# Expert weights passed in 4 MB buffers with a part of all 16 experts each, and 28 blocks of slots instead of 32

## The chip, the cores and the metric

The kernel runs on one core of a Trainium2 chip. Its engines are TensorE (PE, with its weight loads shown apart as PEld), VectorE (DVE), ScalarE (ACT), GpSimd (POOL) and SyncE (SP, which here only issues DMAs). Matmul results land in PSUM (8 banks of 2 KB for each of 128 partitions), everything else sits in SBUF, and all weights come from HBM by DMA. The metric is the device time of one execution in microseconds (us), lower is better.

## The reference, cut to what matters

Two layers act on 256 tokens of width 1024, in fp32. Each layer is a modulated mixer (convolution and two kinds of attention) and a mixture of 16 experts:

```python
for l in range(2):
    mod = silu(c) @ w_ada[l] + b_ada[l]             # 1024 -> 6 x 1024
    sh1, sc1, g1, sh2, sc2, g2 = split(mod, 6)
    h = rms_norm(x, g_mix[l]) * (1 + sc1) + sh1
    x = x + g1 * token_mixers(h, ...)               # w_in: 1024 -> 2340, w_o: 1024 -> 1024
    h = rms_norm(x, g_ffn[l]) * (1 + sc2) + sh2
    aff = sigmoid(h @ w_router); gates = top 2 of 16 experts, both of the best group of 4, normed
    x = x + g2 * sum_e gates[:, e] * ((silu(h @ w_gate[l, e]) * (h @ w_up[l, e])) @ w_down[l, e])
return rms_norm(x, g_final)
```

w_gate and w_up are [2, 16, 1024, 256], w_down is [2, 16, 256, 1024]: 50.3 MB for each layer. Of 256 tokens, 512 pairs of token and expert are routed; an expert can get any number of them. On the inputs that are timed the experts' counts, in units of 32 tokens, exceed one block each for some and two blocks for few.

## The kernel before, in words

**Weights.** All big weight loads stand in one list, `loads`, in the order in which TensorE will use them. `pump` (L72) walks it: while fewer than RING = 14 pieces are issued and not yet freed, it takes a 1 MB tile of the ring and issues the piece's DMAs on SP's queue (L77). `done` (L81) frees a piece after its last matmul and calls `pump` again. The list (L131 to L153) has, for layer 0: sc1 and sh1 (two of the six 4 MB column groups of w_ada, four pieces each), the columns of w_in, g1, sh2, sc2, w_o, g2, then sc1 of layer 1, then the experts, then sh1 of layer 1. An expert load is for a pair of experts: four gate/up pieces of four DMAs of 256 KB (contiguous rows of 1 KB in HBM) and two w_down pieces of two DMAs of 512 KB (rows of 2 KB).

**Order.** The order of the instructions on PE, DVE and ACT is the program's order. `Fill` objects hold matmuls of w_ada (L274, 32 columns of weights and 512 columns wide) that are put into places where TensorE would wait; `take(n)` emits n of its pieces.

**Router.** `route` (L727) forms logits, picks two experts by arithmetic on DVE (L746 to L790), writes the selection `slb`, which TensorE turns into ranks and counts `pk` (L803 to L807). Meanwhile ACT writes the normalised tokens `gH` (rounded) and GpSimd the remainder `gL` (L800). From ranks DVE makes keys `ky`, and a flag per pair.

**Experts.** Slots are in blocks of 32 tokens. A pair of experts has a 128-slot tile of four blocks: block 0 belongs to whichever of the two needs it (its weights are selected by a register, `bass.ds(fr[pr], 1)`, L948), block 1 to the first, blocks 2 and 3 to the second. Eight pairs make 32 blocks. For two pairs at a time, `onehot` (L909) makes the one-hot matrix D, `gather` (L927, matmuls L935) collects the tokens into XT, `weigh` and `onehot_T` (L918) the gate-weighted transpose DT. For each pair, `expert_up` (L951) runs 8 x 4 matmuls with gate and up weights side by side, 512 columns wide (L957; each shows as two instructions), `silu_mul` and `act_T` follow, `expert_down` (L989) runs 2 x 2 x 4 matmuls 512 wide (L995), `put_down` evicts, and `combine` (L1002, matmuls L1016 in the last layer and L1022 in the other) adds the pair's output to PSUM sums. While one pair is in `expert_up`, the DVE, ACT and POOL work of another is under way.

**Overflow.** At the end an `If` (L1169) on a register runs slow extra passes if any pair has more tokens than slots. It stands on PE, ACT, DVE and POOL ahead of the last pair's `combine`; on the timed inputs nothing in it runs. Behind it in layer 0 come the residual and the norm of layer 1 (`nnorm`, with the matmuls of sh1 between), in layer 1 `finish` (L1196: squares, root, scaling, output DMA).

Of the kernel before, what the change touches and what calls it, by code (L numbers as in the profile page):

```python
# [9 lines left out]
F32 = mybir.dt.float32  # L10
# [9 lines left out]
P = 128  # L20
# [13 lines left out]
TAKE = (5, 2)  # L34
# [8 lines left out]
RING = 14  # L43
# [9 lines left out]
def block_kernel(ctx: ExitStack, tc: tile.TileContext, x, c, w_ada, b_ada, g_mix, w_in, w_dw, b_dw, ln_conv_g,  # L53
# [16 lines left out]
    loads, wt, issued, freed = [], {}, [0], [0]  # L70

    def pump(most=RING):  # L72
        while issued[0] < len(loads) and issued[0] - freed[0] < most:
            key, shape, parts = loads[issued[0]]
            t = ring.tile(shape, F32, tag="w", name=f"w{issued[0]}")
            for dst, src in parts(t):
                nc.sync.dma_start(out=dst, in_=src)  # L77
            wt[key] = t
# [32 lines left out]
    def moe_src(l, pr, nm, h, n=2):  # L111
        r = slice(h * (DM // n), (h + 1) * (DM // n))
        if nm == "d":
            src = w_down[l, 2 * pr:2 * pr + 2, :, r].rearrange("e (k p) n -> p e k n", p=P)
        else:
            w = w_gate if nm == "g" else w_up
            src = w[l, 2 * pr:2 * pr + 2, r, :].rearrange("e (k p) f -> p e k f", p=P)
        return [src[:, e] for e in range(2)]

    def add_moe(l):  # L120
        for pr in range(NE // 2):
            for h in range(4):
                srcs = [moe_src(l, pr, nm, h, 4) for nm in "gu"]
                loads.append((("gu", l, pr, h), [P, 2, 2, 2, FE],
                              lambda t, srcs=srcs: [(t[:, e, :, w], srcs[w][e]) for e in range(2) for w in range(2)]))
            for h in range(2):
                srcs = moe_src(l, pr, "d", h)
                loads.append((("d", l, pr, h), [P, 2, 2, 512],
                              lambda t, srcs=srcs: [(t[:, e], srcs[e]) for e in range(2)]))
# [37 lines left out]
    desc4 = cp.tile([P, 4], F32, name="desc4")  # L167
    low4 = cp.tile([P, 4, 4], F32, name="low4")
# [28 lines left out]
    pump(10)  # L197
# [13 lines left out]
    nc.sync.dma_start(out=ropet, in_=rope)  # L211
    nc.sync.dma_start(out=wr[:, :, 0:NE], in_=w_router.rearrange("(k p) e -> p k e", p=P))
    nc.sync.dma_start(out=brt, in_=bass.AP(tensor=b_router.tensor, offset=b_router.offset, ap=[[0, P], [1, NE]]))
    pump()
    G.memset(causal, 0.0)
    for lo in (0, 2 * P):
# [8 lines left out]
           allow_small_or_imprecise_dtypes=True)  # L225
    G.iota(desc4, pattern=[[-1, 4]], base=4, channel_multiplier=0, allow_small_or_imprecise_dtypes=True)
# [89 lines left out]

    class Norm:
# [3 lines left out]
        def tile(self, k):  # L321
            if self.wk is None or k < 2:
                return sm.tile([P, SEQ], F32, name="sq", tag="sq", bufs=2)
            if k >= 6:
                return self.wk.tile([P, FE], F32, name="sq", tag="eac", bufs=2)
            if k % 2 == 0:
                self.two = self.wk.tile([P, 2, SEQ], F32, name="sq", tag="yf")
            return self.two[:, k % 2, :]
# [71 lines left out]
    def mixers(big, wk, l, norm, early):  # L400
# [319 lines left out]
        nxt = Fill([(l, "g2"), (l + 1, "sc1")]) if l + 1 < DEPTH else Fill([(l, "g2")], rows=True)  # L720
# [5 lines left out]

    def route(wk, router, xtp, gH, gL, fill):  # L727
# [3 lines left out]
        part = wk.tile([P, SEQ], F32, name="part", tag="eth", bufs=1)  # L731
# [12 lines left out]
        for t in range(NT):  # L744
# [32 lines left out]
        gtr, eql = (wk.tile([P, FE], F32, name=n, tag="eac")[:, 0:8 * 16].rearrange("p (g a b) -> p g a b", g=8, a=4)  # L777
                    for n in ("gtr", "eql"))
# [4 lines left out]
        ct = wk.tile([P, FE], F32, name="ct", tag="eth", bufs=1)[:, 0:32].rearrange("p (g e) -> p g e", e=4)  # L783
# [7 lines left out]
        fill(2)  # L791
        for h in range(2):
            for t in range(NT):
                hs = slice(h * 512, (h + 1) * 512)
                if t == 0:
                    xs2 = wk.tile([P, NT, 512], F32, name="xs", tag="Yh")
                xs = xs2[:, t, :]
                S.activation(xs, xtp[h, t], AF.Copy, scale=rst[:, t:t + 1])
                S.copy(gH[:, t, hs], xs)
                G.tensor_tensor(gL[:, t, hs], xs, gH[:, t, hs].bitcast(F32), OP.subtract)  # L800
# [7 lines left out]
        npair = NE // 2  # L808
        cnt2 = pk[:, 2, :].rearrange("p (q b) -> p q b", b=2)
        f = tmp([P, npair], "f")  # L810
        V.tensor_scalar(f, cnt2[:, :, 0], BLK + 0.5, None, OP.is_lt)
        fi = wk.tile([1, npair], I32, name="fi", tag="fi", bufs=1)
        V.tensor_copy(fi, f[0:1, :])
# [3 lines left out]
        rk2 = rk.rearrange("p t (q b) -> p t q b", b=2)  # L817
        ky = tmp([P, NT, npair, 4], "ky")
        a32 = tmp([P, NT, npair], "a32", "hi")
        fb = f[:, None, :].to_broadcast([P, NT, npair])  # L820
        V.tensor_scalar(a32, rk2[:, :, :, 0], float(-BLK), None, OP.add)
        dl = tmp([P, NT, npair], "dl", "lo")
        V.scalar_tensor_tensor(out=dl, in0=rk2[:, :, :, 1], scalar=float(-2 * BLK), in1=a32, op0=OP.add,
                               op1=OP.subtract)
        V.tensor_tensor(dl, dl, fb, OP.mult)
        V.tensor_tensor(ky[:, :, :, 0], dl, a32, OP.add)
        V.tensor_copy(ky[:, :, :, 1:3], rk2)
        V.tensor_scalar(ky[:, :, :, 3], rk2[:, :, :, 1], float(-BLK), None, OP.add)

        def gates():  # L830
# [9 lines left out]
            gt2 = gt.rearrange("p t (q b) -> p t q b", b=2)  # L840
            gy = tmp([P, NT, npair, 4], "gy")
            V.tensor_copy(gy[:, :, :, 1:3], gt2)
            V.tensor_copy(gy[:, :, :, 3], gt2[:, :, :, 1])
            nf = tmp([P, npair], "nf", "m1")
            V.tensor_scalar(nf, f, -1.0, 1.0, OP.mult, OP.add)
            V.tensor_tensor(dl, gt2[:, :, :, 1], fb, OP.mult)
            V.tensor_tensor(a32, gt2[:, :, :, 0], nf[:, None, :].to_broadcast([P, NT, npair]), OP.mult)
            V.tensor_tensor(gy[:, :, :, 0], dl, a32, OP.add)
            return gt, gy


        def flags():
            fl = wk.tile([1, 3 * npair + 1], I32, name="flags", tag="flags", bufs=1)
            nb = tmp([P, npair], "nb", "m2")
            V.tensor_scalar(nb, f, float(-BLK), None, OP.mult)
            mx = tmp([1, npair], "mx", "m3")
            V.tensor_tensor(mx, cnt2[0:1, :, 1], nb[0:1, :], OP.add)
            V.tensor_tensor(mx, mx, cnt2[0:1, :, 0], OP.max)
            for ch in range(3):
                V.tensor_scalar(fl[:, ch * npair + 1:(ch + 1) * npair + 1], mx, CAP * (ch + 1) + 0.5, None, OP.is_gt)  # L860
            m1x = tmp([1, 1], "m1x")
            V.tensor_reduce(m1x, mx, AX.X, OP.max)
            V.tensor_scalar(fl[:, 0:1], m1x, CAP + 0.5, None, OP.is_gt)
            return fl, nb

        return ky, gates, flags, rk, fi

    def moe(big, wk, l, router, nxt, nnorm):
        a2, sh2 = mod["sc2", l], mod["sh2", l]
        npair = NE // 2  # L870
        last = l + 1 == DEPTH
        if last:

            g2b = big.tile([P, DM], F32, name="g2b")
            o2 = l * 6 * DM + UNITS.index("g2") * DM
            nc.sync.dma_start(out=g2b, in_=bass.AP(tensor=b_ada.tensor, offset=b_ada.offset + o2,
                                                   ap=[[0, P], [1, DM]]))
        g2ps = []

        def spread_g2():  # L880
            for h in range(2):
                pb = bank([P, 512])
                T.matmul(pb, selu[:, 0, h:h + 1].to_broadcast([P, P]), nxt.groups[0].ev, start=True, stop=True)
                g2ps.append(pb)

        gH = big.tile([P, NT, DM], F32R, name="gH")
        gL = big.tile([P, NT, DM], F32R, name="gL")
        xtp = {}

        def fill(i):  # L890
            if i > 1:
                nxt.take(TAKE[i - 2])
                if i == 3 and last:
                    spread_g2()
                return
            for h, t in ((0, 0),) if i == 0 else ((0, 1), (1, 0), (1, 1)):
                pt = bank([P, 512])
                for j in range(4):
                    xk = xT[:, 4 * h + j, t * P:(t + 1) * P]
                    if last:  # L900
# [408 lines left out]
```

## Time and profile before

| | before |
|---|---|
| median of 3 runs | 592.75 us (591.54 to 592.85) |
| profiled execution, time | 592.18 us |
| profiled execution, span | 590.5 us |
| PE busy | 548.6 us, 93% |
| DVE busy | 277.8 us, 47% |
| ACT / POOL busy | 157.6 us, 27% / 46.0 us, 8% |
| DMA moved | 182.82 MB, mean 310 GB/s; SP's queue 88.2% of 16 engines' span |

The span runs from the first to the last record of the execution, and the time is 1.68 us longer. Times below are us from the span's start. The stages of the span: layer 0's mixers to about 159, its router to 181, its experts to 296, the overflow branch, residual and norm to 314; layer 1's mixers to 438.8, its router to 460.2, its experts to 575.2, then the end. In a row, "idle before <-releaser" is the time for which the engine stood still just before the instruction, and what ended it; a name that ends in q (PEq) is that engine's instruction queue.

### The profile page before, as it was taken

To read this page: it belongs to the slowest core of one execution; us is meant where nothing else is said; L and a number is where in the kernel's file an instruction comes from. 1 tells how busy PE (TensorE), PEld (TensorE's weight loads), DVE (VectorE), ACT (ScalarE), POOL (GpSimd) and SP (SyncE) were. 2 spreads that over 40 slices of the span, in tenths; PEclk is the share of its full clock that TensorE was granted. 3 is DMA by queue.
4 is the path that set the end of the run, shared out by engine and by line. 5 is a ranking of instruction groups with operands and counts; after the bars stand their busy time and mean duration, and the time that the engine had idled before them with its cause. 6 is when DMAs were issued, how large, how long until landed. Compare 5 with 4: busy or idle time off the path is not lost. (4 is left out here: it accounts for less than half of the span.)

```text
span 590.5 us, 10358 instructions
## 1 busy us (share of the span) xinstructions
PE 548.6 (93%) x3881; PEld 336.7 (57%) x3881; DVE 277.8 (47%) x882; ACT 157.6 (27%) x368; POOL 46.0 (8%) x51
## 2 busy tenths in 40 slices
PE   2889999999979999999969999999997999999993
PEld 0378886677735444444337788668774554444331
DVE  1321999574264433332133099956427533333222
ACT  1331103346242111111134021344624211111114
POOL 1000004000030000000000000500003011111110
PEclk9979999999989999999979999999998999999997
DMA  8999989973499999999999997957349699999932
GB/s 320 383 302 380 401 316 394 398 268 116 140 335 363 363 363 354 359 348 359 391 352 372 384 383 308 347 196 246 122 143 332 199 360 361 359 363 361 356 112 75
DMA packets 126025, 182.82 MB, mean 310 GB/s; under 512 B 7920, under 2 KB 94216, under 8 KB 125960
## 3 DMA queue, kind: packets, MB, share of 16 engines
q1 hardware_dynamic: 125344, 180.80, 88.2%
q10 hardware_dynamic: 616, 1.19, 0.5%
q8 instruction: 36, 0.59, 0.4%
q14 instruction: 29, 0.24, 0.1%
HBM read 180.92 MB, written 1.05 MB: 308 GB/s over the span
## 5 line engine op out<-in xcount | busy, mean ns | idle before, releaser
L957 PE MATMUL bank<-w,XT 128*32 128x512 f32 (+1 forms) x1024 | 112.9, 592 | 0.0
L431 PE MATMUL bank<-w,hT 128*128 128x256 f32 (+1 forms) x448 | 102.9, 390 | 1.1 <-ACT hT L407 1.1
L431 PEld LDWEIGHTS bank<-w,hT 128*128 128x128 f32 x448 | 85.6, 193 | 16.9 <-ACT hT L407 2.1
L957 PEld LDWEIGHTS bank<-w,XT 128*32 128x32 f32 x1024 | 33.6, 110 | 75.1 <-issue 69.3
L995 PE MATMUL bank<-w,eaT 128*32 128x512 f32 (+1 forms) x512 | 58.2, 595 | 0.4
L645 PE MATMUL bank<-yT,w 128*128 128x256 f32 x256 | 57.5, 381 | 0.0
L274 PE MATMUL bank<-w,cB 128*32 128x512 f32 x384 | 50.8, 641 | 5.7 <-DMA w<-in_w_ada 3.5
L645 PEld LDWEIGHTS bank<-yT,w 128*128 128x128 f32 x256 | 48.0, 190 | 6.8 <-issue 0.7
L674 DVE SCALAR_TENSOR_TENSOR cvy<-cva,hw,cvy 128x256 f32<-128x256 f32 x108 | 49.7, 509 | 0.6
L945 DVE SCALAR_TENSOR_TENSOR eac<-eth,bank 128x256 f32<-128x256 f32 x16 | 6.7, 421 | 83.5 <-ACT eth L944 83.5
L935 PE MATMUL bank<-D,gH 128*128 128x256 f32 x128 | 33.1, 297 | 2.4 <-DVE eac L945 2.4
L995 PEld LDWEIGHTS bank<-w,eaT 128*32 128x32 f32 x512 | 15.2, 110 | 32.0 <-issue 28.9
L944 ACT ACTIVATE eth<-bank 128x256 f32<-128x256 f32 x16 | 6.1, 384 | 96.2 <-PE bank L957 96.2
L935 PE MATMUL bank<-D,gL 128*128 128x256 f32 x128 | 31.2, 282 | 0.0
L939 ACT ACTIVATE XT<-bank,sh,sc 128x256 f32<-128x256 f32 x36 | 18.2, 560 | 44.4 <-PE bank L935 44.4
L935 PEld LDWEIGHTS bank<-D,gH 128*128 128x128 f32 x128 | 24.7, 193 | 6.7 <-issue 4.7
L446 PE MATMUL bank<-hT,w 128*128 128x256 f32 x128 | 28.3, 379 | 0.0
L446 PEld LDWEIGHTS bank<-hT,w 128*128 128x128 f32 x128 | 24.2, 190 | 3.3
L274 PEld LDWEIGHTS bank<-w,cB 128*32 128x32 f32 x384 | 10.6, 112 | 26.7 <-issue 16.5
L983 POOL TENSOR_TENSOR Yl<-yf,Yh 128x512 fp32r<-128x512 f32 x14 | 18.0, 1283 | 95.1 <-ACT Yh L982 95.1
L522 ACT ACTIVATE pr<-pr,nm 128x128 f32<-128x128 f32 (+1 forms) x48 | 21.3, 444 | 14.1 <-DVE nm L519 14.1
L935 PEld LDWEIGHTS bank<-D,gL 128*128 128x128 f32 x128 | 24.7, 193 | 0.2 <-issue 0.2
(268 smaller groups left out, 662.9 us busy)
## 6 DMA issues: line engine op xcount, KB each, us to landing
w<-in_w_ada SPq DMA_DIRECT2D x48, 1024.0 KB, 11.6
w<-in_w_gate SPq DMA_DIRECT2D x128, 256.0 KB, 6.1
w<-in_w_up SPq DMA_DIRECT2D x128, 256.0 KB, 5.9
w<-in_w_down SPq DMA_DIRECT2D x64, 512.0 KB, 7.5
w<-in_w_in SPq DMA_DIRECT2D x16, 1024.0 KB, 13.0
w<-in_w_o SPq DMA_DIRECT2D x8, 1024.0 KB, 9.1
w<-in_w_in SPq DMA_DIRECT2D x4, 328.0 KB, 15.8
xin<-in_x ACTq DMA_DIRECT2D x1, 1024.0 KB, 9.4
```

The lines of the kernel that those rows point to most:

```text
L274: T.matmul(self.pa[j:j + 32, :], cB[:, 2 * kq + kk, o:o + 32], W[:, kk, h * 512:(h + 1) * 512], start=(u == 0 and kq == 0), stop=(u + 1 == ...
L431: T.matmul(pts[t], hT[:, k, tt], W[:, kk, :], start=first, stop=last)
L446: T.matmul(pp[:, cc, :], W[:, kk, cs], hT[:, k, :], start=(k == 0 and cc == 0), stop=(k == KT - 1 and cc == 1))
L522: S.activation(pr[:, lo:hi], pr[:, lo:hi], AF.Exp, bias=nm[:, u:u + 1], scale=-1.0, accum_out=sums[:, u:u + 1])
L645: T.matmul(pos[n // 2][:, n % 2, :], W[:, n * P:(n + 1) * P], yT[:, k, :], start=(ki == 0 and n % 2 == 0), stop=(ki == KT - 1 and n % 2 == 1))
L674: tap = V.scalar_tensor_tensor(out=cy[:, cc, :], in0=src, scalar=w, in1=cy[:, cc, :], op0=OP.mult, op1=OP.add)
L935: T.matmul(pg[:, i, :], z[:, t, ks], D[:, t, :], start=(si == 0), stop=(si == 3))
L939: S.activation(XT[:, k, :], pg[:, i, :], AF.Identity, bias=sh2[:, k:k + 1], scale=a2[:, k:k + 1])
L945: V.scalar_tensor_tensor(out=ac, in0=th, scalar=1.0, in1=pgu[:, 0, :], op0=OP.add, op1=OP.mult)
L957: T.matmul(pf[b0:b0 + BLK, :], XT[:, k, o + b0:o + b0 + BLK], W[:, e, k % 2, :], start=(k == 0), stop=(k == KT - 1))
L983: (V if whole else G).tensor_tensor(Yl[:, sl], yf, Yh[:, sl].bitcast(F32), OP.subtract)
L995: T.matmul(pd[b0:b0 + BLK, :], aT[:, f, b0:b0 + BLK], W[:, e, f, :], start=(f == 0), stop=(f == 1))
```

## The change

RING becomes 4 buffers of 4 MB (32 KB for each partition). `pack` puts the pieces of `loads` into these in order; a buffer is freed when all its pieces are done, and only then is the buffer four places further on issued. For the experts each buffer holds one part of all 16: eight buffers for gate and up (for each quarter `kp` of the 1024 input rows one with w_gate, one with w_up; two input rows per partition, contiguous runs of 2 KB) and four for w_down (a quarter `c` of the output columns each, runs of 1 KB at a pitch of 4 KB), each of four 1 MB DMAs. Since two neighbouring input rows now lie in one partition, `reorder` brings the modulation into the same order, and gH and gL are written in it. sh1 of layer 1 is loaded ahead of layer 0's experts, and its matmuls go to the router's fill. Three small DMAs of the start (ropet, wr, brt) move from SP's queue to ACT's; gL's subtraction moves from GpSimd to DVE.

There are 28 blocks: one for each of 16 experts, a second one for experts 0, 3, 6, 9, 12, and seven that go to whichever experts need them. They stand in seven groups of four (`q`); a group's block 0 is one of the seven, with its expert in a register. `more_blocks`, a chain on DVE, counts what each expert needs beyond its own blocks, and finds the owner of each of the seven and the keys of its slots. All gate and up sums of a layer stay in seven PSUM banks while the eight buffers go by; the gather for the next quarter stands between the matmuls of this one. Matmuls are 256 columns wide. After the eight buffers, SiLU and transposes for all groups, then the four w_down buffers with evictions (`put_down`) and `combine` two steps behind. All of `combine` now stands ahead of the overflow `If`. The core of the diff:

```diff
-RING = 14
+RING = 4
+RTILE = 8192
+XB = 7
+SECOND = (0, 3, 6, 9, 12)
     def done(*keys):
         for key in keys:
             del wt[key]
-            freed[0] += 1
+            left[owner[key]] -= 1
+            freed[0] += left[owner[key]] == 0
         pump()
+    def up_src(w, l, e0, n, kp):
+        return w[l, e0:e0 + n, 256 * kp:256 * (kp + 1), :].rearrange("e (p k) f -> p e (k f)", k=2)
+    def down_src(l, e0, n, c):
+        return w_down[l, e0:e0 + n, :, 256 * c:256 * (c + 1)].rearrange("e (k p) n -> p (e k) n", p=P)
...
-            add_ada(l + 1, "sc1")
+            add_ada(l + 1, "sc1", "sh1")
         add_moe(l)
-        if l + 1 < DEPTH:
-            add_ada(l + 1, "sh1")
+    pack()
...
-    nc.sync.dma_start(out=ropet, in_=rope)
+    nc.scalar.dma_start(out=ropet, in_=rope)
...
-                G.tensor_tensor(gL[:, t, hs], xs, gH[:, t, hs].bitcast(F32), OP.subtract)
+                V.tensor_tensor(gL[:, t, hs], xs, gH[:, t, hs].bitcast(F32), OP.subtract)
...
+        def expert_up(w, kp, kk):
+            W = wt[w, l, kp]
+            for q in range(NQ):
+                for j in range(4):
+                    e, i, b = block(q, j)
+                    T.matmul(sums(w, q)[BLK * j:BLK * j + BLK, :], XT[kp, i][:, kk, BLK * b:BLK * b + BLK],
+                             W[:, e, kk, :], ...)
...
+        gather_set(0, 0, (0, 1))
+        gather_set(0, 1, (0, 1))
+        nxt.take()
...
+        gather_set(0, 3)
+        own, kx, ei, x_, bg, bx = more_blocks()
+        onehot(kx, D[2][:, :, 0:BLK * XB], XB, BLK)
+        gather_set(0, 2)
+        reg += nc.values_load_multi_w_load_instructions(ei[0:1, 0:XB], engines=(ET.PE,), min_val=0, max_val=NE - 1)[1]
...
+        def turn(d):                       # d: two groups q (the last: one)
+            GD = u([P, NT, n, P], "GD")
+            for qi in range(n):
+                ...                        # weigh(...) for each run of blocks of one D, and for block 0
+            onehot_T(GD..., n, DT[d], gate[d])
+        def silu1(d):
+            S.activation(th, g_u("g", d), AF.Tanh, scale=0.5)
+            V.scalar_tensor_tensor(out=ac[d], in0=th, scalar=1.0, in1=g_u("g", d), op0=OP.add, op1=OP.mult)
...
+        for kp in range(4):
+            for w in "gu":
+                for kk in range(2):
+                    expert_up(w, kp, kk)
+                    if kp < 3:
+                        gather_set(kp + 1, (0, 1, 2, 3)[2 * (w == "u") + kk])
+                done((w, l, kp))
+                ...
+                if kp == 3 and w == "g":
+                    for d in range(4):
+                        silu1(d)
+                        turn(d)
...
+        for c in range(4):
+            for d in range(4):
+                expert_down(c, d)
+                late.append((c, d))
+                if len(late) > 2:
+                    combine(*late.pop(0))
+            done(("d", l, c))
+        for x in late:
+            combine(*x)
         with tc.If(anyov[0]):
```

## Rows read from the trace of the kernel before

**Rows 1.** Stages: length, busy time (instructions) by engine, granted clock, DMA share, GB/s.
```profile
181.30:296.30 115.00, 113.56 (x1009) 52.52 (x1008) 39.22 (x88) 20.41 (x37) 0.00 (x0) 1.00 1.07 362
314.00:438.80 124.80, 124.77 (x706) 97.33 (x707) 75.80 (x282) 38.81 (x105) 7.54 (x6) 1.00 0.78 277
460.20:575.20 115.00, 113.60 (x953) 49.73 (x952) 41.07 (x87) 19.57 (x38) 17.96 (x14) 1.00 0.95 316
```

**Rows 2.** SP's queue in order of time: the first expert load of layer 0.
```profile
117.17 1.13 SPq L77 DMA_DIRECT2D w<-in_w_gate  x1
```

**Rows 3.** PE in order of time, router of layer 0: start, us, instruction, count.
```profile
159.91 0.62 PE L388 MATMUL bank<-xT,wrp 128*32 128x256 f32 x8
160.34 0.61 PE L392 MATMUL bank<-sq,msel 128*32 128x256 f32 x8
...
164.41 4.50 PE L274 MATMUL bank<-w,cB 128*32 128x512 f32 x40
172.87 0.17 PE L803 MATMUL bank<-slb,tri 128*128 128x16 bf16 x1 [3.96 <-DVE slb L787]
...
177.11 0.28 PE L935 MATMUL bank<-D,gH 128*128 128x256 f32 x1
177.23 0.28 PE L935 MATMUL bank<-D,gL 128*128 128x256 f32 x1
...
181.29 7.07 PE L957 MATMUL bank<-w,XT 128*32 x64
```

**Rows 4.** Short stretches read for the DMA rate, columns as in rows 1.
```profile
183.00:192.00 9.00, 7.74 (x73) 3.84 (x66) 4.09 (x21) 1.57 (x4) 0.00 (x0) 1.00 1.10 350
213.00:216.00 3.00, 3.00 (x32) 0.91 (x28) 0.26 (x1) 0.00 (x0) 0.00 (x0) 1.00 1.05 384
57.00:69.00 12.00, 12.00 (x68) 10.12 (x67) 10.91 (x48) 3.21 (x7) 0.00 (x0) 1.00 1.03 410
27.00:36.00 9.00, 6.77 (x30) 4.88 (x30) 3.90 (x12) 3.88 (x9) 0.00 (x0) 0.68 0.99 261
```

**Rows 5.** All engines in order of time, end of layer 0's experts.
```profile
292.68 3.64 PE L995 MATMUL bank<-w,eaT 128*32 x32
300.00 0.55 PE L1022 MATMUL bank<-DT,Yh 128*128 128x256 f32 x1 [3.68 <-PEq L1169]
303.69 0.11 DVE L594 MEMSET cva<- 128x60 f32 x1 [5.83 <-DVEq L1169]
307.96 0.48 DVE L396 SCALAR_TENSOR_TENSOR xT<-bank,g,xT 128x256 f32<-128x256 f32 x1 [0.38 <-issue]
```

**Rows 6.** All engines in order of time, hand-over to layer 1's mixers.
```profile
311.27 1.05 PE L285 MATMUL bank<-selu,adaev 128*128 128x2 f32 x8 [0.17 <-ACT adaev L279]
```

**Rows 7.** DVE by line and shape, 173 to 300: count, busy us, mean ns, idle before.
```profile
L924 DVE TENSOR_SCALAR DT<-bank 128x512 fp32r<-128x512 f32 x4 | 2.8, 692 | 0.1
L946 DVE SCALAR_TENSOR_TENSOR eac<-eac,bank 128x256 f32<-128x256 f32 x8 | 3.4, 420 | 0.3
L835 DVE TENSOR_TENSOR gt<-aff,sl 128x32 f32<-128x32 f32 x1 | 0.2, 191 | 0.0
```

**Rows 8.** All engines in order of time, router of layer 1.
```profile
446.82 5.17 POOL L800 TENSOR_TENSOR gL<-xs,gH 128x512 fp32r<-128x512 f32 x4 [67.48 <-DVE gs L769]
...
448.05 0.28 DVE L779 TENSOR_TENSOR eql<-bi 128x128 f32<-128x128 f32 x1
448.25 1.35 DVE L780 TENSOR_TENSOR gtr<-bi 128x128 f32<-128x128 f32 x1
...
452.50 0.19 DVE L787 SCALAR_TENSOR_TENSOR slb<-ct,ing 128x32 bf16<-128x32 f32 x1
```

**Rows 9.** All engines in order of time, end of the kernel.
```profile
577.01 0.47 PE L1016 MATMUL bank<-Yh,DT 128*128 128x512 f32 x1 [1.85 <-PEq L1169]
...
578.39 1.28 ACT L258 ACT_TABLE_LOAD   x1 [3.40 <-ACTq L1169]
579.89 0.58 ACT L1202 ACTIVATE fsq<-bank 128x512 f32<-128x512 f32 x1
```

More of the change, by code (lines that the diff above doesn't have):

```diff
@@ L892, in fill @@
                 nxt.take(TAKE[i - 2])
+                if i == 2:
+                    reorder()
                 if i == 3 and last:
-                    spread_g2()
+                    for h in range(2):
+                        pb = bank([P, 512])
+                        T.matmul(pb, selu[:, 0, h:h + 1].to_broadcast([P, P]), nxt.groups[0].ev, start=True, stop=True)
+                        g2ps.append(pb)
                 return
@@ L898, in fill @@
                 for j in range(4):
[L899 to L903 removed]
+                    T.transpose(pt[:, j * P:(j + 1) * P], xT[:, 4 * h + j, t * P:(t + 1) * P], ident)
                 xtp[h, t] = pt
[L906 to L907 removed]
+        rk, rks, more_blocks, gates, flags_ = route(wk, router, xtp, gH, gL, fill)
         def onehot(key, D, nb, w):
@@ L989, in expert_down @@
-        def expert_down(pr, gate, aT, Yh, Yl):
-            for h in range(2):
-                W = wt["d", l, pr, h]
-                pd = bank([P, 512])
-                for f in range(2):
-                    for b0, e in blocks(pr):
-                        T.matmul(pd[b0:b0 + BLK, :], aT[:, f, b0:b0 + BLK], W[:, e, f, :], start=(f == 0),
-                                 stop=(f == 1))
-                done(("d", l, pr, h))
-                put_down(pd, gate, h, Yh, Yl)
-        accs = [xtp[h, t] for t in range(NT) for h in range(2)] if last else []
@@ new lines, in expert_down @@
+        def expert_down(c, d):
+            W = wt["d", l, c]
+            n = 2 if d < 3 else 1
+            pd = bank([P, n, 256])
+            for qi in range(n):
+                for f in range(2):
+                    for j in range(4):
+                        js = slice(BLK * j, BLK * j + BLK)
+                        T.matmul(pd[js, qi, :], aT[d][:, qi, f, js], W[:, block(2 * d + qi, j)[0], f, :],
+                                 start=(f == 0), stop=(f == 1))
+            Y[c, d] = u([P, n, 256], "Yh", F32R), u([P, n, 256], "Yl", F32R)
+            put_down(pd, gate[d], c, *Y[c, d], n)
@@ new lines, in add_block @@
+        def add_block(c, DTb, yh, yl, first=False):
+            for z in (yh, yl):
+                for i in range(2):
+                    if last:
+                        T.matmul(accs[c // 2, i][:, (c % 2) * 256:(c % 2 + 1) * 256], DTb[:, i * P:(i + 1) * P], z,
+                                 start=False, stop=False, skip_group_check=True)
+                    else:
+                        T.matmul(accs[c][:, i, :], z[:, i * P:(i + 1) * P], DTb, start=(first and z is yh and i == 0),
+                                 stop=True, skip_group_check=True)
@@ L1037, in moe, with combine @@
+        def combine(c, d):
+            if not last and d == 0:
+                accs[c] = bank([P, 2, SEQ])
+            for qi in range(2 if d < 3 else 1):
+                add_block(c, DT[d][:, qi, :], Y[c, d][0][:, qi, :], Y[c, d][1][:, qi, :], d == 0 and qi == 0)
         engs = (ET.PE, ET.Activation, ET.DVE, ET.Pool)
         def extra(pr, ch, tiles):
-            x8, oD, oGD, oDT, rc, ogate, th, ac, aT, Yh, Yl = tiles
-            oXT, wbuf = x8[:, 0:KT // 2, :].rearrange("p a (b n) -> p (a b) n", b=2), x8[:, KT // 2:, :]
@@ L1074, in extra @@
-            combine(oDT[:, 0, :], Yh, Yl)
-            if ch < 2:
+            for wi, w in enumerate((w_gate, w_up)):
+                for kp in range(4):
+                    W = fetch(kp % 2, lambda e: up_src(w, l, e, 1, kp)[:, 0, :])
+                    for kk in range(2):
+                        for j in range(2):
+                            T.matmul(pgu[64 * j:64 * j + 64, wi, :],
+                                     oX[kp // 2][:, 2 * (kp % 2) + kk, 64 * j:64 * j + 64],
+                                     W[j][:, kk * FE:(kk + 1) * FE], start=(kp == 0 and kk == 0),
+                                     stop=(kp == 3 and kk == 1))
```

588 lines of the change are left out of this document (287 added, 301 removed).

## The prediction

> **What bounds the kernel now.** I read the page first (PE 93% busy, SP's queue 88%: two resources near their limit), then the stages, then the order of time on SP and on PE around the experts, last the small rows. In the stages [rows 1] PE is busy for 113.6 of 115 us of either layer's experts and for 124.77 of 124.8 us of the mixers. But look at the DMA column: 1.07 in layer 0's experts, 0.95 in layer 1's, 0.78 in the mixers. In the mixers transfers wait for PE; in layer 0's experts both are full. So whatever the change takes from PE there is worth nothing unless the transfers end earlier too, and when these may begin counts. Before, the first expert load is issued at 117.17 [rows 2], 64 us ahead of the first expert matmul at 181.29 [rows 3].
>
> **When the transfers of layer 0 begin.** Packed in order, buffers 8 to 11 hold the last half of w_o, g2, and sc1 and sh1 of layer 1; the first gate buffer is the twelfth, and needs buffer 8 back, which holds two pieces of w_o and half of g2. g2's first pieces are used at about 159, the second stands at the head of the 40 L274 instructions at 164.41 [rows 3]; 8 instructions of 0.107 us later, at 165.4, it is free. Before, some 6 MB of experts lie in SBUF by then; after, none.
>
> **Their rate.** In stretches of one kind of load [rows 4]: rows of 1 KB 350 GB/s (DMA share 1.10), rows of 2 KB (w_down before) 384, rows of 4 KB (w_ada) 410. Gate and up now come in runs of 2 KB: 4.194 MB / 384 = 10.92 us a buffer; w_down in runs of 1 KB: 4.194 / 349 = 12.02. Twelve buffers: 8 x 10.92 + 4 x 12.02 = 135.5 us. From 165.4, with an estimate of 1.5 us from issue to the flow and 1.0 for the last completion, the last buffer lands at 303.4. Bounds: all at 350 gives 311.6, all at 410 gives 290.6.
> The rows say that the rate follows the length of a run, though all these DMAs move 256 to 1024 KB. The Trainium skill ("DMA: Bandwidth & Descriptors", Bandwidth) ties it to the size of a DMA instead: 1 MB 341, 16 MB 425 GB/s. By the best of these the 50.3 MB would take 118 us and land at 286, by the 1 MB figure 147.5 us and 315; no row shows either as a rule, and the 256 KB DMAs at 350 speak against size alone.
>
> **PE, layer 0.** A group of four blocks, 256 wide, is 8 instructions. L388 and L392 have this form (32 columns of weights, 256 wide, fp32), and follow each other in 0.43 us for 8 [rows 3]: 53.6 ns each. L957 at 512 wide has 7.07/64 = 110 ns [rows 3], so half the width costs half the time. A buffer is 28 blocks x 2 matmuls x 2 instructions = 112 x 53.6 ns = 6.0 us; with two gathers of 8 matmuls at 0.117 us (177.11 to 177.23 [rows 3]) 7.9. Six of these, two of 6.0, four down buffers of 6.0 and 112 combine matmuls of 0.117 (13.1) make some 97 us, with transposes and first gathers 105, against 115. That is the saving of the 28 blocks: 10 us a layer.
> Two DVE chains stand in its way. (1) `more_blocks`, 16 operations of 0.19 to 0.42 us (128x32 and 128x256 [rows 7]) = 5.2 us, then one-hot, gather, eviction and seven register loads, all ahead of the first expert matmul. Before that the route is shorter by 3.6 us (below), but gL takes 4 x 0.69 = 2.8 of DVE, and three g2/sc1/sh1 pieces are taken ahead of it. I get a first expert matmul at about 191.5 for 181.3; one more piece in the router's fill lies in an idle stretch of 3.96 us (172.87 [rows 3]). (2) Between the last gate buffer and the last up buffer stand `silu1` and `turn` of all four d in PE's order: 14 `weigh` operations (4.4 us), SiLU's 4 (3 x 0.69 + 0.42 = 2.5), DT and its sum (3 x 1.37 + 0.8 = 4.9; a 128x512 operation is 0.69 [rows 7]), and 2 us for ACT's start and hand-overs: about 14 us in which PE has only 14 transposes. Cover-free it costs 14, at best 0.
> Gate 3 can't start before its buffer lands at 244 (165.4 + 1.5 + 7 x 10.92) and is done at 250; up 3 after the chain at 270 to 272, while w_down goes on loading. PE's own chain would end at 311.5. The transfers': last buffer 303.4, its 112 instructions 6.0, combines left 4.7: 314.1. So the transfers decide, by 2.6.
>
> **From there to layer 1.** Before, the `If` held DVE for 5.83 us (303.69 [rows 5]), with half of the last combine behind it, and the residual ended at 308.4 (307.96 + 0.48). After, no matmul is behind it, but the wait remains: DVE's last eviction 313.1 + 5.8 + 8 x 0.42 = 322.3, later by 13.9. sh1's matmuls no longer stand in the norm; its row transposes there took 1.05 [rows 6], so I give back 1.2 (0 to 2). Layer 0: **+12.7** (bounds: with 410 GB/s PE decides, +10; with 350, +21; with 410 and chain (2) hidden, -4). The mixers of layer 1 stay bound by PE, so this moves through undiminished.
>
> **Layer 1.** In before's time: GpSimd's gL runs for 5.17 us beside DVE, and the same 128x128 operation takes 1.35 there for 0.28 just before [rows 8]; over the four hurt operations some 3.6 us, which the move to DVE gives back, so slb (452.50) is ready at 449. The rest as in layer 0, less the g2/sc1/sh1 pieces: first expert matmul at about 465 for 460.2 [rows 1]. Four expert buffers can be issued before it (their predecessors are freed from 396 to 448); the fifth needs gate 0 done, 465 + 7.9 + 2 for a lower granted clock after the waits = 474.8. From 476.3, 4 x 10.92 + 4 x 12.02 = 91.8: landed at 569 with completion, end of the sums 579.7. PE: gate 3 done at 520, chain (2) to 534, up 3 to 540, SiLU, transposes and the re-transpose of x to 546, four down buffers and combines 37.3: **583.5**. Here PE decides. Before, ACT's table load came at 578.39, 3.2 after the last expert matmul (575.2), by the `If` [rows 9]; after it comes at 586.7, and the first square at 588.2 for 579.89 [rows 9]. Since all sums are then complete, `finish` loses two waits (1.2 together): **+7.1** (chain (2) hidden: +3.4; transfers at 410 too: -7).
>
> **Start.** ropet, wr and brt are small descriptors; a stretch with them shows 261 GB/s for 350 to 410 [rows 4], 2 to 3 us of transfer time. On ACT's queue they run beside the first w_ada loads, on which PE waits: +1.0 (0 to 2.3).
>
> **Sum.** Span 590.5 + 1.0 + 12.7 + 7.1 = 611.3; with the 1.7 outside the span 613.0 for the profiled execution, which stands 0.6 below the median of the runs. I say 613.
>
> **The rivals.**
> (a) *PE's saving decides* and it gets faster. For it: PE is 98.7% busy in these stages, the saving is 10 us a layer, DVE is at a third there [rows 1]. It needs transfers at 410 GB/s in both layers (from 165.4 they must land by 290.7 only to break even) and chain (2) under cover. Then layer 0 gives -3.9 and layer 1 -6.8: 592.2 - 10.7 + 0 to 1 = about 582; from some 400 GB/s on (125.8 us of transfers: layer 0 +3, layer 1 -4) it is no slower than before. Against: no row of 1 or 2 KB runs is above 384, and the program's order puts chain (2) in front of up 3. 13%.
> (b) *PE's issue decides*: an instruction costs what it did at 512 wide (110 ns, 592 ns busy), and twice as many are as slow. 1344 instructions a layer x 56 ns more = 76 us a layer; less the 2.6 of slack in layer 0, 613 + 149 = 762 at most, 688 at half of that. L388 and L392 speak against it, but none of their weights is picked by a register. 5% for such an end, 8% for one between.
> The Trainium skill ("TensorE: Matmul & The Clock Gate", Wait — 56ns, not 53.3ns?) has a cost of about 62 ns for a matmul when hardware decode is off. By it a layer's 1344 instructions take 11 us more, layer 0 +9 (PE then decides), layer 1 +11: an estimate of 633, the middle case of (b). The 53.6 ns of L388 disagree.
> (c) *Only the transfers decide*, chain (2) hidden: layer 1 +3.4: 609. This is my forecast with one term gone; 20%, the forecast itself 44%.
> (d) *Worse transfers*: w_down's 1 KB runs at a 4 KB pitch, not seen before, are slower than contiguous ones, or four big buffers starve a stage that 14 small ones fed. At 300 GB/s w_down takes 7.9 more a layer: layer 0 +7.9, layer 1, where PE had 3.8 in hand over the transfers, +4: 625. 10%.
> (e) *The overflow runs*, so that 28 blocks don't do what they say: that costs hundreds of us. With the timed inputs 3 and 5 of the seven movable blocks are needed in the two layers, counted from the reference's routing; excluded.
>
> **Numbers.** A measurement of this kernel tells a change from none at about 0.3% (1.8 us). Faster (a) 13%, same 4% (between a and c), slower 83%. The likeliest case with (c) spans 604 to 622; the range that leaves out 20% reaches 598 to 635.
>
> **What would show it.** Right: gate 0's first DMA of layer 0 at about 165, the last w_down landing at 300 to 305, DMA share over 1 in between and PE with gaps; a gap of 10 us or more on PE before the last up buffer, released by DVE; groups of 8 instructions in 0.43 us; layer 1's last combine about 8 us after the last before. Wrong: gate 0 issued well ahead of 165, rates of 400 for 2 KB runs, no such gap, or a slower pace of L957's successor.

## The result, and the profile after

The changed kernel takes 633.72 us (median of 4 runs, 632.48 to 634.52) for 592.78 before: a ratio of 1.0694, 95% interval 1.0672 to 1.0716, 41 us slower. The forecast was 613 in a range of 598 to 635: the direction held, the size was half. The profiled execution has a span of 632.7.

Page of the changed kernel, parts 1 and 3 (before: 548.6 us of PE, 93%, and 88.2% for q1, in the table ahead):
```profile
PE 552.7 (87%) x5081; PEld 380.3 (60%) x5081; DVE 280.8 (44%) x950; ACT 161.4 (26%) x380; POOL 17.9 (3%) x33
q1 hardware_dynamic: 103760, 179.62, 79.4%
```
PE does as much work as before in a span 42 us longer, and the transfers' share fell as well. So neither is fuller than before; both wait. Stages of the changed kernel, columns as in [rows 1]: layer 0's router up to the first expert matmul, its experts up to the last combine, the hand-over to layer 1's mixers, then layer 1's router, experts and end.
```profile
162.90:197.50 34.60, 22.89 (x202) 12.90 (x202) 15.90 (x61) 11.52 (x24) 0.00 (x0) 0.82 0.81 298
197.50:323.80 126.30, 117.74 (x1580) 74.66 (x1580) 35.22 (x93) 23.77 (x48) 0.00 (x0) 0.96 1.06 367
323.80:339.40 15.60, 7.27 (x31) 3.12 (x31) 6.28 (x19) 5.52 (x15) 0.10 (x1) 0.64 1.08 353
...
465.30:493.40 28.10, 15.63 (x138) 9.88 (x139) 15.58 (x57) 11.60 (x24) 0.00 (x0) 0.86 0.81 292
493.40:620.30 126.90, 118.90 (x1612) 75.20 (x1612) 44.79 (x111) 19.61 (x36) 0.00 (x0) 0.94 0.81 276
620.30:632.70 12.40, 0.00 (x0) 0.00 (x0) 3.25 (x8) 5.77 (x14) 0.00 (x0) 0.70 0.24 89
```
Beside 98.7% in [rows 1], PE is busy for 93% of the experts' stages, at a clock of 0.94 to 0.96. The same points read from both kernels' PE rows, us from the span's start:

| point on PE | before | after | delay | forecast of the delay |
|---|---|---|---|---|
| end of layer 0's w_o | 159.0 | 162.9 | +3.8 | +1.0 |
| first expert matmul | 181.3 | 197.5 | +16.2 | +11.2 |
| last combine | 307.0 | 323.8 | +16.8 | |
| layer 1's first projection | 314.0 | 339.4 | +25.3 | +13.7 |
| end of layer 1's w_o | 438.8 | 465.3 | +26.6 | +13.7 |
| first expert matmul | 460.2 | 493.4 | +33.2 | +18.5 |
| last combine | 583.5 | 620.3 | +36.8 | |
| end of the span | 590.5 | 632.7 | +42.2 | +20.8 |

The waits of PE in the changed kernel (total us, times, longest) name three places, all on DVE:
```profile
PE bank L1000 <- DVE D L976: 17.8, 5, 6.2
PE bank L989 <- DVE GD L981: 14.2, 6, 2.5
PE bank L300 <- DVE cB L265: 8.3, 1, 8.3
```

**The start**, all engines in order of time:
```profile
9.17 0.42 DVE L250 TENSOR_TENSOR low<-it 128x256 f32<-128x256 f32 x1
...
16.37 0.17 DVE L1340 TENSOR_SCALAR brt<-brt 128x16 f32<-128x16 f32 x1 [6.78 <-DMA brt<-in_b_router]
16.45 0.16 DVE L264 SCALAR_TENSOR_TENSOR ca<-cth,par 128x8 f32<-128x8 f32 x1
16.65 0.17 DVE L265 TENSOR_SCALAR cB<-ca 128x8 f32<-128x8 f32 x1
16.88 1.94 PE L300 MATMUL bank<-w,cB 128*32 128x512 f32 x8 [8.31 <-DVE cB L265]
```
L1340 stands a thousand lines behind L265 in the program, and L265 makes the operand of the first w_ada matmul. Here DVE's order isn't the program's (on DVE it is only in the experts' part, unlike what I wrote under "Order"): a planner writes it. With brt's DMA on ACT's queue it put L1340 first, and DVE stood for 6.78 us behind a DMA that nobody needs before the router.

**The first experts of layer 0** (PE): the last gather waits 6.19 for the chain of L850 to L877. The first expert matmul's row names w_gate, but that buffer, issued at 169.38, is in long before: its packets have all arrived by 181.8. What stands there is the last gather's way through ACT and DVE, whose last eviction ends at 196.8; in E10b, with the buffer loaded 21 us earlier, the same 1.9 us stand at this place.
```profile
193.56 0.55 PE L1000 MATMUL bank<-D,gH 128*128 128x256 f32 x1 [6.19 <-DVE D L976]
...
197.51 5.40 PE L1044 MATMUL bank<-w,XT 128*32 x56 [1.91 <-DMA w<-in_w_gate]
202.84 0.38 PE L1000 MATMUL bank<-D,gH 128*128 128x256 f32 x1
```
**The end of layer 0's experts**, all engines: everything behind the `If` starts 5 us after PE's last combine; before, half of the last combine and of the residual ran beside that [rows 5].
```profile
323.35 0.40 PE L1176 MATMUL bank<-DT,Yl 128*128 128x256 f32 x2
328.59 1.28 ACT L284 ACT_TABLE_LOAD   x1 [6.82 <-ACTq L1264]
328.81 3.23 DVE L425 SCALAR_TENSOR_TENSOR xT<-bank,g,xT 128x256 f32<-128x256 f32 x8 [6.52 <-PEq L1264]
330.54 1.06 PE L365 MATMUL bank<-sq,mean_d 128*32 128x256 f32 x3 [6.79 <-ACT sq L363]
```

### The profile page after: what moved, and what is told of

Same layout as the page of the kernel before. It is cut to its first block, busy times and chain, and to the rows that moved or that the text cites. A ratio compares the mean times of both kernels' runs of the same rounds, so it can differ in the third digit from the quotient of the medians.

```text
span 632.7 us, 12552 instructions
## 1 busy us (share of the span) xinstructions
PE 552.7 (87%) x5081; PEld 380.3 (60%) x5081; DVE 280.8 (44%) x950; ACT 161.4 (26%) x380; POOL 17.9 (3%) x33
## 5 line engine op out<-in xcount | busy, mean ns | idle before, releaser
L1044 PE MATMUL bank<-w,XT 128*32 128x256 f32 (+1 forms) x1792 | 112.9, 400 | 5.2 <-DMA w<-in_w_up 2.2
L1044 PEld LDWEIGHTS bank<-w,XT 128*32 128x32 f32 x1792 | 60.9, 115 | 47.6 <-issue 15.1
L1007 DVE TENSOR_SCALAR XT<-bank,mp 128x256 f32<-128x256 f32 (+1 forms) x28 | 14.1, 504 | 104.4 <-ACT XT L1004 104.4
L1164 PE MATMUL bank<-w,aT 128*32 128x256 f32 (+1 forms) x896 | 54.9, 382 | 0.6 <-issue 0.6
L1004 ACT ACTIVATE XT<-bank,mp 128x256 f32<-128x256 f32 (+1 forms) x36 | 18.8, 540 | 129.9 <-PE bank L1000 129.9
L1000 PE MATMUL bank<-D,gH 128*128 128x256 f32 (+1 forms) x128 | 36.0, 314 | 17.8 <-DVE D L976 17.8
L1164 PEld LDWEIGHTS bank<-w,aT 128*32 128x32 f32 x896 | 26.5, 109 | 19.3 <-issue 1.4
L1000 PE MATMUL bank<-D,gL 128*128 128x256 f32 (+1 forms) x128 | 33.3, 292 | 0.0
L300 PEld LDWEIGHTS bank<-w,cB 128*32 128x32 f32 x384 | 10.9, 113 | 29.9 <-issue 21.1
L1145 DVE SCALAR_TENSOR_TENSOR Yl<-bank,gate,Yh 128x256 fp32r<-128x256 f32 x28 | 13.5, 483 | 29.4 <-ACT Yh L1144 29.4
L425 DVE SCALAR_TENSOR_TENSOR xT<-bank,g,xT 128x256 f32<-128x256 f32 x24 | 10.2, 478 | 32.1 <-PE bank L674 25.6
## 6 DMA issues: line engine op xcount, KB each, us to landing
w<-in_w_gate SPq DMA_DIRECT2D x32, 1024.0 KB, 12.6
```

Source lines behind the costliest of these rows:

```text
L300: T.matmul(self.pa[j:j + 32, :], cB[:, 2 * kq + kk, o:o + 32], W[:, kk, h * 512:(h + 1) * 512], start=(u == 0 and kq == 0), stop=(u + 1 == ...
L1000: T.matmul(pg[:, i, :], z[:, t, ks], D[:, t, 0:n], start=(si == 0), stop=(si == 3))
L1004: S.activation(XT[:, i, 0:n], pg[:, i, :], AF.Identity, bias=mp[:, 1, k:k + 1], scale=mp[:, 0, k:k + 1])
L1007: V.tensor_scalar(XT[:, i, 0:n], pg[:, i, :], mp[:, 0, k:k + 1], mp[:, 1, k:k + 1], OP.mult, OP.add)
L1044: T.matmul(sums(w, q)[BLK * j:BLK * j + BLK, :], XT[kp, i][:, kk, BLK * b:BLK * b + BLK], W[:, e, kk, :], start=(kp == 0 and kk == 0 and ( ...
L1145: V.scalar_tensor_tensor(out=Yl[:, qi, :], in0=pd[:, qi, :], scalar=gates_[:, qi:qi + 1], in1=Yh[:, qi, :].bitcast(F32), op0=OP.mult, op1= ...
```

## The experiments

Times are medians, ratios against the kernel before on the same chip; the changed kernel's is 1.0694 (1.0672 to 1.0716). A difference to the changed kernel is one of medians taken on different chips. By the ratios it is 5.6 us for E1, 10.8 for E2, 9.1 for E3, 3.3 for E4, 10.3 for E5, 14.3 for E9 and 10.2 for E10b, each known to some 2 us.

**E1, brt's DMA back on SP; E8, brt's DMA alone on ACT in the kernel before.**
```diff
-    nc.scalar.dma_start(out=brt, in_=...)
+    nc.sync.dma_start(out=brt, in_=...)
```


> The changed kernel with brt's DMA alone back on SP's queue; ropet and wr stay on ACT's. In its trace the first w_ada matmul waits 8.31 us for cB, and DVE stands 6.78 us ahead of cB for brt's DMA, which the order of DVE's instructions put there. Theory (that one wait is the start's loss): the first w_ada matmul is back at 9 to 10 us, the end of layer 0's mixers at 159 to 160 for 162.9, the time 3 to 4 us below 633.7, so 629.7 to 630.7. Rival (my prediction's reason: small descriptors beside the w_ada loads): two of three small DMAs stay where they are, the gain is under 1.5 us.

627.91 us, ratio 1.0599 (1.0564 to 1.0635): 5.8 less, more than expected. The first w_ada matmul is at 10.52, w_o's end at 157.8 (159.0 in the kernel before, so ropet and wr, still on ACT's queue, cost nothing that shows). E8 is the same word the other way:

> The kernel before with brt's DMA alone on ACT's queue, one word of the change. Theory (DVE's order): cB waits for brt here too, the first w_ada matmul comes at 15 to 17 us instead of 9.3 and the time rises by 2 to 4 us, to 595 to 597. Rival (transfer time of small descriptors): one DMA of 64 bytes a partition moves nothing by more than 0.5 us.

601.07 us, 1.0127 (1.0096 to 1.0158): 8.4 more, twice what was expected. DVE of E8:
```profile
8.95 0.22 DVE L223 CAST tri<-trif 128x128 bf16<-128x128 f32 x1
21.76 0.17 DVE L1257 TENSOR_SCALAR brt<-brt 128x16 f32<-128x16 f32 x1 [12.59 <-DMA brt<-in_b_router]
```
Removed in one kernel and put into the other, the wait moves the start both ways. It is shown: what the start lost is the place in DVE's order of an instruction that waits for brt, not transfer time taken from the w_ada loads.

**E2, turn(d) spread over the last two buffers.**
```diff
                     if kp < 3:
                         gather_set(kp + 1, ...)
+                    else:
+                        turn((0, 1, 2, 3)[2 * (w == "u") + kk])
...
                     for d in range(4):
                         silu1(d)
-                        turn(d)
```


> The changed kernel with turn(d) of the four d put behind the four half buffers of the last gate and up buffers, one each, instead of all four ahead of the last up buffer; the same instructions. PE now waits 7.1 us a layer there for DVE's GD, besides 3 us of transposes at a low rate and a lower granted clock behind it. Theory (this DVE chain is on PE's path, and PE, not the transfers, ends layer 0's experts): 6 to 9 us less in layer 1 and 5 to 6 in layer 0, where the last buffer's landing at about 307 then binds; the time 620 to 623. Rival (the transfers end layer 0, as I predicted): layer 0's last combine stays at 323.7 and only layer 1 gains, 625 to 628.

622.80 us, 1.0511 (1.0493 to 1.0530): 10.9 less. In layer 1 first expert matmul to last combine takes 119.6 for 126.9. In layer 0 up 3 ends 9.8 earlier, but the last combine only 3.2, for 5 to 6 expected, and 1.6 of these were there at the first expert matmul. Two of PE's rows there:
```profile
284.67 3.08 PE L1165 MATMUL bank<-w,aT 128*32 x32 [3.25 <-DMA w<-in_w_down]
...
308.37 1.93 PE L1165 MATMUL bank<-w,aT 128*32 x32 [0.64 <-DMA w<-in_w_down]
```
So the transfers stand about 3 us behind PE: in the changed kernel PE decided layer 0, and with this chain gone they do.

**E3, the block-finding chain ahead of the first gathers.**
```diff
+        own, kx, ei, x_, bg, bx = more_blocks()
+        onehot(kx, D[2]...); onehot(rks..., D[2]...); onehot(rks..., D[3]...)
         gather_set(0, 0, (0, 1))
         gather_set(0, 1, (0, 1))
         nxt.take()
         gather_set(0, 3)
-        own, kx, ei, x_, bg, bx = more_blocks()
         gather_set(0, 2)
```


> The changed kernel with the DVE chain that finds the seven movable blocks (and its one-hots) put ahead of the first gathers and of the w_ada fill instead of behind them; the same instructions. PE waits 6.2 us a layer for it and starts the experts at a lower clock. Theory (chain on PE's path): first expert matmul 7 to 8 us earlier in layer 0 and 4 to 6 in layer 1; of layer 0's gain 6 remain, because the landing of the last buffer binds then; together 9 to 12, time 622 to 625. Rival (the first expert matmul waits for its buffer, which lands just before it: the trace shows a wait of 1.9 for w_gate and of 2.2 for w_up): not above 4 us.

626.05 us, 1.0540 (1.0497 to 1.0583): 7.7 less, for 9 to 12 expected. Layer 0's first expert matmul is at 187.3 (10 earlier), its last combine at 320.9, again 3 earlier: the same floor as E2. That the experts can start 10 earlier answers the rival: they weren't waiting for their buffer. Layer 1's router is 2.9 shorter, less than expected.

**E4, combine in batches of four.**
```diff
-                if len(late) > 2:
-                    combine(*late.pop(0))
+                if len(late) > 4:
+                    for _ in range(4):
+                        combine(*late.pop(0))
```


> The changed kernel with combine done in batches of four behind the next w_down's first group, instead of one after each group: the same matmuls, a quarter of the switches between expert_down and combine. In the changed kernel's trace 32 expert_down instructions take 1.86 us to the next combine and 8 combine matmuls 1.14 to the next expert_down, 0.34 more than the two pure prices (1.72 and 0.94). Theory (a switch between the two kinds costs, and my sum left it out): 12 pairs of switches a layer less, 4 us a layer, time 625 to 627. Rival (the instructions themselves are slower, by their narrowness or their registers): no change beyond 1 us.

628.95 us, 1.0638 (1.0612 to 1.0663): 4.8 less. The w_down phase shrinks from 43.5 to 40.5 us in layer 0 (with a wait of 1.3 for w_down that is new) and from 42.2 to 39.3 in layer 1. The edit takes away 10 pairs of switches a layer and not 12, since the last combines stood together before as well (14 places become 4): 0.3 us for each pair. In the changed kernel (PE) 32 instructions take 1.86 to the next kind:
```profile
303.86 1.93 PE L1164 MATMUL bank<-w,aT 128*32 x32
305.72 0.51 PE L1176 MATMUL bank<-DT,Yh 128*128 128x256 f32 x2
306.06 0.40 PE L1176 MATMUL bank<-DT,Yl 128*128 128x256 f32 x2
306.39 1.95 PE L1164 MATMUL bank<-w,aT 128*32 x32
```
In E4 a whole buffer, 112 instructions and 28 combines, takes 596.04 - 586.32 = 9.72 for 10.69:
```profile
586.32 6.25 PE L1164 MATMUL bank<-w,aT 128*32 x112
592.50 0.50 PE L1173 MATMUL bank<-Yh,DT 128*128 128x256 f32 x2
...
596.04 6.25 PE L1164 MATMUL bank<-w,aT 128*32 x112
```
**E7, a fixed expert for block 0.**
```diff
-            return bass.ds(reg[q], 1), 2, q
+            return 2 * q, 2, q
```


> The changed kernel with a fixed expert (2q) for the weights of each group's block 0 in place of the register; the register loads stay. It leaves out that the seven movable blocks use their own expert's weights. Theory (registers cost PE nothing: 56 ns an instruction with them, 53.6 without in rows of this form): under 1.5 us. Rival (b of the prediction, PE's issue decides, one register operation for every four matmuls now, twice as many as before): 10 to 25 us.

626.79 us, 1.0595 (1.0573 to 1.0617): 6.9 less, 5.9 by the ratios, more than expected and less than the rival's. The profile is of the shortest of five executions (622.10; the others took 626.57 to 627.63), and w_o's end, ahead of anything that the edit touches, is at 158.9 in it for 162.9, so its span says little of what the edit is worth. Layer 1 hardly moves (126.1 us from first expert matmul to last combine for 126.9; its gate/up phase 78.7 in both). In layer 0 that phase is 77.7 for 81.2: in the changed kernel PE stalls in each of five buffers there, for 0.5 to 0.8 us in four and 1.2 in the last gate buffer, as in the first row (PE, the first half of the second gate buffer), and in none in E7, as in the second. But E10b below has the registers, and there too the same half buffer runs without a stall, as in the third:
```profile
216.80 3.88 PE L1044 MATMUL bank<-w,XT 128*32 x56
```
```profile
211.66 3.23 PE L1044 MATMUL bank<-w,XT 128*32 128x256 f32 x56
```
```profile
210.90 3.23 PE L1046 MATMUL bank<-w,XT 128*32 x56
```
Four of the five stalls are gone in E10b. So the registers alone don't make them, and what does stays open. As a pace, PE's issue is not the bound: 112 instructions in 6.18 us are 55 ns each, also with registers. The 62 ns that the Trainium skill has ("TensorE: Matmul & The Clock Gate", Wait — 56ns, not 53.3ns?) for decode without hardware is not seen; that the estimate from it, 633, lies beside the 633.72 measured is chance.

**E5, the changed kernel without the overflow If; E6, the kernel before without it.**
```diff
-        with tc.If(anyov[0]):
-            for p2 in range(npair):
-                if_over(p2, 0, tiles)
```


> The changed kernel without the overflow If; it leaves out the overflow path, of which nothing runs on these inputs. In its trace layer 0's residual starts 5.06 us behind the last combine matmul's start window and ACT's table load 6.8 us behind ACT's last work; at the end the first square stands 3.6 us behind the last combine. Theory (all engines meet at the If behind PE's last combine, so all of it is on the path): 4 to 5 us in layer 0 and 3 to 4 at the end, 7 to 9 together, 625 to 627. Rival (the residual's and norm's own chain is what is long): under 4.

> The kernel before without the overflow If, again only the path is left out. There the If stands ahead of the last pair's combine: PE waits 3.7 us for it in layer 0 and 1.85 at the end, ACT 5.1 and 3.4, half of it beside combines. Theory (the change made the If dearer by moving combine ahead of it): 3 to 6 us together here, 2 to 5 less than in the changed kernel, time 587 to 590. Rival (the If costs the same in both): 7 to 9, time 584 to 586.

E5: 622.76 us, 1.0520 (1.0495 to 1.0545), 11 less. E6: 584.13, 0.9875 (0.9855 to 0.9895), 7.6 less. E5 missed: the If costs more than I thought. E6 came out at its rival's time, though not for the rival's reason: by the ratios the If costs 10.3 us behind `combine` and 7.4 ahead of the last one, 3 more (known to some 2). In E5 (all engines) the residual runs into the last combines, and the hand-over takes 6.9 us for 15.6:
```profile
323.23 3.22 DVE L425 SCALAR_TENSOR_TENSOR xT<-bank,g,xT 128x256 f32<-128x256 f32 x8
...
324.37 0.40 PE L1176 MATMUL bank<-DT,Yl 128*128 128x256 f32 x2
```
**E10b, sh1 of layer 1 put back behind the experts; E9, E1 to E4's edits together; E10, these and sh1 back.**
```diff
-            add_ada(l + 1, "sc1", "sh1")
+            add_ada(l + 1, "sc1")
         add_moe(l)
+        if l + 1 < DEPTH:
+            add_ada(l + 1, "sh1")
...
-        nxt = Fill([(l, "g2"), (l + 1, "sc1"), (l + 1, "sh1")]) ...   # TAKE = (6, 2)
+        nxt = Fill([(l, "g2"), (l + 1, "sc1")]) ...                   # TAKE = (5, 2); sh1 in the residual
```


> The changed kernel with sh1's load and matmuls put back behind layer 0's experts, nothing else. My prediction's step (the transfers decide layer 0 by 2.6, so a buffer more ahead is worth 10 us): 9 to 11 us less, minus 2 to 3 for sh1's matmuls in the norm: 625 to 627. New theory (PE decides layer 0, with the transfers 3 us behind it; PE's own chain has one w_ada piece less ahead of the experts): last combine 1 to 3 us earlier, given back in the norm: 631 to 635.

623.83 us, 1.0522 (1.0494 to 1.0549): 9.9 less, as my prediction's step would have it and three times what the new theory gave. But not by that step: PE waits nowhere for w_down, and it wasn't the transfers that freed it (first row, PE: no buffer is named; the wait is as long as in the changed kernel). The first expert matmul comes at 192.1 for 197.5 (the fill of sh1, its eviction and its row transposes stood on PE and DVE ahead of the block-finding chain), and from there to the last combine it takes 122.8 for 126.3: up to chain (2) 59.9 for 63.5, with four of the stalls of E7's first row gone (one is left, in the second row: 6.90 us for 6.25). sh1's matmuls in the residual cost nothing: 15.9 for 15.6 to the first projection.
```profile
192.08 4.92 PE L1046 MATMUL bank<-w,XT 128*32 x56 [1.90 <-issue]
...
245.12 6.90 PE L1046 MATMUL bank<-w,XT 128*32 x112
```

> The changed kernel with four of the edits together: brt's DMA on SP, the block-finding chain first, turn(d) spread over the last gate and up buffers, combine in batches of four. Theory (PE's waits and switches cost what the single runs showed, and in layer 0 the landing of the last buffer then binds): layer 0's start 5 us earlier, last combine of layer 0 at 315 to 316 for 323.75, not below, with PE waiting for w_down; in layer 1 3 us of the router, 8 to 9 of the last up buffer, 3 of w_down's phase; time 608 to 612. Rival (nothing but PE counts, gains add up in layer 0 too): 597 to 602.

618.24 us, 1.0452 (1.0419 to 1.0485): 15.5 less, where the four alone gave 29. PE's waits on DVE fall from 42 to 16 us, and new ones for transfers appear:
```profile
PE bank L1165 <- DMA w<-in_w_down: 8.4, 4, 4.1
PE bank L1000 <- DVE D L976: 8.2, 3, 4.0
```
Layer 0's last combine is at 319.5, 4 later than I expected; the issue of the first gate buffer moved only from 169.4 to 166.4, and 152 to 153 us lie between the two in E2, E3 and E9 alike (154.4 in the changed kernel). That is the transfers' floor.

> The kernel with these four edits, and sh1 of layer 1 loaded behind layer 0's experts as before the change, its matmuls behind the If. Then the first gate buffer is the eleventh, and waits for buffer 7 (half of sc2 and two pieces of w_o), which is free before the router. Theory (the transfers bind layer 0 there from the point on at which the first buffer is freed): the first gate DMA issued 12 us or more earlier, the last w_down lands about 11 us earlier, last combine of layer 0 7 to 11 us earlier until PE binds; of this 2 to 3 are lost again to sh1's matmuls in the norm; time 600 to 604. Rival (PE binds layer 0 also here): no gain beyond 2 us, or a loss.

606.73 us, 1.0233 (1.0205 to 1.0262): 11.5 less than E9. The first gate load is issued at 145.50 for 166.38, and layer 0's last combine comes 10.5 earlier. The mechanism holds, the sum is 3 above the range: layer 1's router and the hand-overs keep their price. Against the kernel before, E10 reaches the last combine of layer 0 2.0 later, and its layer 1 experts take 118.3 us for 123.3: there the rebuilt loop is the faster one at last. 13.5 of the 14.2 us that are left in its span lie in the two stretches behind the last combine (15.0 for 7.0, 12.7 for 7.1).

**E12, the kernel before with the If ahead of the last pair's expert_up.**
```diff
         for pr in range(npair):
+            if pr == npair - 1:
+                ...                        # anyov, tiles
+                with tc.If(anyov[0]): ...
             expert_up(...)
...
-        with tc.If(anyov[0]): ...
```


> The kernel before with the overflow If moved from behind the last pair's expert_down to ahead of its expert_up; nothing left out. Leaving the If out altogether was worth 7.6 us there. Theory (the meeting of all engines at the If costs most where ACT and DVE have the next work of the path; ahead of expert_up PE alone loses its drain and restart, 3.7 us as in layer 0 before): 2 to 4 us less, 588.5 to 590.5. Rival (a restart of PE costs its lower granted clock as well, wherever it stands): no change within 1 us, or slower.

605.56 us, 1.0218 (1.0186 to 1.0251): 13 slower. My theory missed; the rival's "or slower" came true. PE and all engines meet there too, and PE waits for the restart of others, 7.6 us in layer 0 and 5.9 in layer 1. All engines, layer 0:
```profile
290.86 1.28 ACT L258 ACT_TABLE_LOAD   x1 [5.92 <-ACTq L1137]
291.78 9.86 PE L957 MATMUL bank<-w,XT 128*32 x64 [7.60 <-DVEq L1137]
...
301.74 1.28 ACT L944 ACT_TABLE_LOAD   x1 [9.29 <-issue]
```
These 64 instructions take 9.86 us for 7.07 [rows 3], at a granted clock of 0.71. And on ACT the load of the table for the norm (L258) now comes ahead of the last pair's SiLU, which loads its own back (L944), so that the norm's is loaded once more: two more loads of 1.28 us a layer. E12 has the price of the place and of this together. No version here that keeps the overflow path beats the kernel before.

## Why the prediction was wrong

**Right.** The first gate load waits for buffer 8 (165.4 plus the start's delay is 169.2; it came at 169.38). The rates: 385 GB/s for the 2 KB runs in the stretch 213 to 257 and 348 for the 1 KB runs in 281 to 306, for 384 and 349 [rows 4]; the first buffer was in 12.4 us after its issue, as forecast, and the last one in E2 139.8 us after the first issue, for 138.0. So of the two readings the length of a run gave the rate, and not the size of the DMA, since all these DMAs are of 1 MB. The Trainium skill ("DMA: Bandwidth & Descriptors", Bandwidth) has 341 GB/s for a DMA of 1 MB, issued from GpSimd; both rates here are above it. gL's move gave what was forecast: from the first selection step (bi) to slb layer 0's router takes 3.4 us for 7.4 on DVE, and the operation that took 1.35 beside GpSimd's gL [rows 8] takes 0.28. Chain (2) stood on PE: 10.3 us in layer 0 and 10.6 in layer 1 for 14. Rivals (a), (d) and (e) did not happen; (b) by its pace neither.

**Wrong: "So the transfers decide, by 2.6."** PE decided layer 0 (E2, E3), because PE's chain, from which also layer 1's 583.5 came, was too short: 126.9 us from the first expert matmul to the last combine in layer 1 for 118.5. Piece by piece there: gate and up to chain (2) 60.7 for 55, chain (2) 10.6 for 14, up 3 7.4 for 6.0, w_down 42.2 for 37.3. The price of an instruction was right within 2 ns; what I left out is what lies between: the switch between 32-column fp32 matmuls and gathers or combines (E4: 0.3 us a pair, 14 pairs in w_down's phase; the 12 pairs of the gate/up phase show the same 0.3, from one half buffer with its gathers to the next 4.30 us for 3.08 and 0.94) and the lower granted clock behind each wait, which I had charged once (the first half buffer takes 5.40 in layer 0 and 5.95 in layer 1 for 3.23, up 3's 112 instructions 7.4 for 6.2). Multiplying pure prices gave a saving of 10 us a layer; the kernel before had its switches and waits inside the 115 us that I compared with.

**Wrong: the start, +1.0 for +3.8.** I priced transfer time; what the changed queue moved was the planner's order on DVE (E1, E8).

**Wrong: sh1, -1.2.** I counted its departure from the norm, where it cost nothing, and folded its arrival into the first expert matmul; E10b gives 9.9 us for the whole move. The first expert matmul came 5.0 later than forecast in layer 0, of it 2.8 by the start, and 1.8 later in layer 1's router.

**Wrong: the hand-over.** From the last combine to layer 1's first projection 15.6 us; my steps give 12.6. The norm's squares and sums now all come behind the residual, at a clock of 0.64, with nothing beside them. In E3 and E9 the same instructions take 13.9 us, at 0.74 and 0.72: 1.7 of the 3.0 go with the clock.

The sum: +2.8 start, +8.8 layer 0 (8.4 of PE's chain less the 2.6 by which I had let the transfers decide, 3.0 hand-over), +1.3 layer 1's mixers (from the first projection to the router's first matmul 126.9 for 125.6; the experiments spread from 125.6 to 127.1, so it isn't told from none), +8.5 layer 1. 21.4 of 42.2 in all.

**Open:** what stalls layer 0's gate/up phase (E7, E10b). No run separates the 28 blocks, the narrower matmuls and the 4 MB buffers from each other.

## What to carry to other kernels

Where a stage shows both PE and the transfers full, a coarser buffer pays twice: its first load waits for its last user, and the work between buffers comes in blocks that nothing covers. Price a rebuilt loop from rows that contain its switches and its waits with the clock behind them, not from single instructions, and look at where every small instruction of a moved DMA ends up in an order that a planner writes. Where a branch stands that all engines share is worth a run: 7.6 us went to one here that never runs, and both other places tried were dearer, the one in E12 together with more table loads. No run found a better one.

## What the runs showed of the hardware that was not expected

Two branches not taken, one a layer, cost 7.6 us in the kernel before and 11.0 (10.3 by the ratio) in the changed one. A row of E8: one small DMA, issued at 7.2 beside the first w_ada loads, landed only at 21.8. And a switch between the two kinds of matmul took 0.3 us a pair with nothing waiting.
